# In the final projection x is added behind the joins instead of ahead of them, and the first gate block takes its units in another order

## The chip, the core and the metric

The kernel runs on one core of a Trainium2 chip. The metric is device time in microseconds: 2481.99 us, the median of three runs (2481.8 to 2482.37). One further execution was profiled; its trace is read below. TensorE (PE) multiplies matrices and loads weights beside that (PEld), VectorE (DVE) and ScalarE (ACT) do elementwise work, GpSimd (POOL) and SyncE (SP) only issue transfers in the part that matters here.

## The reference

One decoder layer on x (256 tokens, 4096 channels), in float32. What matters here are its last steps:

```python
proj = rmsnorm(h, g_pre) @ w_in          # ..., merge_a, merge_b are the last 2 x 4096 columns
...
merged = sigmoid(merge_a) * (o_a @ p_a) + sigmoid(merge_b) * (o_b @ p_b)
h = h + merged @ w_o                     # the final projection: x is added to it
```

## The kernel before

Every float32 product is made of three passes: both operands are split into a high part, which ACT rounds to the matmul type (`whi`, `whs`), and a low part, which DVE gets by subtraction (`wlo`, `wls`); PE then multiplies high by high, low by high and high by low (`mm3`, lines 106 to 108).

The second half of the kernel ("wide") streams the merge gates' columns of w_in, then p_a and p_b, then w_o. It goes in blocks of 1024 output columns: seven gate blocks, four blocks each of p_a and p_b, and four of w_o (cb = 0 to 3). A block's inner dimension is cut into 16 pairs of 128-row tiles, and each pair is one unit. A unit `p5` multiplies pair 5 plainly: 24 matmuls, one split of 2048 columns on DVE. A unit `s4` multiplies pair 4 in Winograd's way: 21 matmuls, but DVE first makes sums of weights (lines 1231 to 1233) and has more to split. `k1` or `k14` is no matmul: it packs the left operand of a pair, that is, makes the sums that the s units of that pair need, and overwrites a part of the pair's operand by a difference (`pack`, lines 1088 to 1098). After its pack the pair can't be multiplied plainly any more.

A list written by hand gives the order of the units of each block; `mixed` is the usual one. Work is emitted with a look-ahead: before PE's unit i come the splits of unit i+2 (`prep`), and the loads of units i+3 to i+5 on the SP queue into three buffers `wraw`. The split tiles `whi` and `wlo` have three buffers too. Each engine executes its own list in order.

A block fills eight accumulator banks of 512 columns: four for plain and late Winograd products (`c`), four for the Winograd products that several outputs share (`s`). Consecutive blocks swap the two sets. After the block's last s unit `sums_early` combines the s banks into four SBUF tiles `ev`, one per quarter of the output. After the last unit the c banks are added to them by a join: ACT copies a bank to a tile `evc` (two buffers) and POOL issues a transfer that accumulates it into `ev` (lines 1301 and 1302). The join of the quarters 0 follows the last unit's first half, the join of the quarters 1 comes two units later. The next block's first s unit needs the banks that this frees: it is the third unit (`p3 p5 s0`).

In the gate blocks `ev` then goes through a sigmoid and is stored. In the w_o blocks x is added: `add_x` (line 1385) issues on POOL's queue a transfer that accumulates 128x512 of x from HBM into `ev`. It stands at the end of `sums_early`, so ahead of the joins of the same four tiles; accumulations into one tile go one after another. `finish` (three units after the block's end) stores the four tiles, on POOL too. The last w_o block has no join: DVE adds the bank (`sum_late`) and SP stores.

Of the kernel before, what the change touches and what calls it, by code (L numbers as in the profile page):

```python
# [37 lines left out]
def kernel(ctx: ExitStack, tc: tile.TileContext, x, positions, g_pre, w_in, g_q_lat,  # L38
# [1004 lines left out]
    QUARTERS = [(m, h) for m in range(2) for h in range(2)]  # L1043
# [88 lines left out]
    def block(w, c0, order, end, npairs=16, base=0, sets="cs"):  # L1132

        seq = [(u[0], int(u[1:])) if isinstance(u, str) else u for u in order]
        b = {"w": w, "c0": c0, "end": end, "base": base, "sets": sets, "on": set(), "c": None, "s": None, "ev": None}
        prods = [i for i, u in enumerate(seq) if u[0] in "sp"]
        last_s = max([i for i in prods if seq[i][0] == "s"], default=None)
        for i, (kind, p) in enumerate(seq):
            sched.append({"kind": kind, "p": p, "b": b if kind in "sp" else None, "last_s": i == last_s,
                          "last": i == prods[-1]})  # L1140
# [22 lines left out]
    def raw_dma(i):  # L1163
        if i >= len(sched) or i in asked:
            return
        asked.add(i)
        u = sched[i]
        kind, p, b = u["kind"], u["p"], u["b"]
        if kind not in "spgm":
            return  # L1170
        t = raws[i] = wraw()
        if kind in "gm":
            src = go_d[p // 2][:, 8 * (p % 2):8 * (p % 2) + 8, :] if kind == "g" else mt_d[:, 8 * p:8 * p + 8, :]
            nc.sync.dma_start(flat(t), src.rearrange("p k t -> p (k t)"))
            return
        for kk in range(2):
            q = 1 - kk if kind == "s" else kk
            row = (2 * p + kk) * P
            nc.sync.dma_start(flat(t[:, 2 * q:2 * q + 2, :]), b["w"][row:row + P, b["c0"]:b["c0"] + 1024])
# [103 lines left out]
    def sums_early(b):  # L1283
        e = b["ev"] = ev_tiles()
        s = b["s"]
        v = nc.vector.tensor_tensor
        nc.scalar.copy(e[0, 0], s["p1"])
        v(e[0, 1], s["p6"], e[0, 0], op=ALU.add)
        v(e[1, 0], s["p7"], e[0, 1], op=ALU.add)
        v(e[0, 1], s["p5"], e[0, 1], op=ALU.add)  # L1290
        v(e[1, 1], s["p5"], e[1, 0], op=ALU.add)

    def sum_late(b, m, h, cs=slice(0, 512)):
        e = b["ev"][m, h]
        nc.vector.tensor_tensor(e[:, cs], b["c"][m, h][:, cs], e[:, cs], op=ALU.add)

    def join(b, m):

        for h in range(2):
            t = F["pb"].tile([P, 512], F32, name="evc", bufs=2)  # L1300
            nc.scalar.copy(t, b["c"][m, h])
            nc.gpsimd.dma_start(b["ev"][m, h], t, accum_op=ALU.add)
# [4 lines left out]
    def end_sig(d, c0):  # L1307
        def end(b):
            def finish(m):
                for h in range(2):  # L1310
                    e = b["ev"][m, h]
                    nc.scalar.activation(e, e, AF.Sigmoid, scale=r[:, m:m + 1])
                    nc.gpsimd.dma_start(sig_d[d][m * P:(m + 1) * P, c0 + 512 * h:c0 + 512 * h + 512], e)

            later.append((2, lambda: join(b, 1)))
            later.append((3, lambda: finish(0)))
            later.append((5, lambda: finish(1)))
        return end
# [3 lines left out]
    for n, (d, cb) in enumerate(gates):  # L1322
        order = mixed
        if n == 0:
            order = "p3 p5 s0 p7 s2 p9 k1 s4 p11 s6 s8 p13 s10 s1 s12 s14 p15".split()
        if n == len(gates) - 1:
            order = mixed[:15] + ["g0", "p15"]
        block(w_in, (C_MA, C_MB)[d] + 1024 * cb, order, end_sig(d, 1024 * cb), sets=("cs", "sc")[n % 2])
# [24 lines left out]
    def transpose_merged(cb):  # L1353
        banks = bank_set("c")
        e = F["merged"]
        t = F["merged_t"] = F["pb"].tile([P, 4, 512], F32, name="mt")
        for j2 in range(4):
            for a in range(2):
                for m in range(2):
                    j = 2 * j2 + a  # L1360
                    nc.tensor.transpose(banks[j2][:, a * S + m * P:a * S + (m + 1) * P],
                                        e[m, j // 4][:, (j % 4) * P:(j % 4 + 1) * P], ident)
            nc.scalar.copy(t[:, j2, :], banks[j2])
        if cb < 3:
            nc.gpsimd.dma_start(mt_d[:, 8 * cb:8 * cb + 8, :].rearrange("p k t -> p (k t)"), flat(t))
# [15 lines left out]
    def at_out(ap, c0, m, h):  # L1381
        return ap[m * P:(m + 1) * P, c0 + 512 * h:c0 + 512 * h + 512]

    def add_x(b, m, h):
        nc.gpsimd.dma_start(b["ev"][m, h], at_out(xf, b["c0"], m, h), accum_op=ALU.add)

    def end_out(b):
        def finish():
            for q in QUARTERS:
                nc.gpsimd.dma_start(at_out(of, b["c0"], *q), b["ev"][q])  # L1390

        later.append((2, lambda: join(b, 1)))
        later.append((3, finish))

    for cb in range(4):
        order = mixed
        if cb == 0:
            order = "p3 p5 t3 p7 p9 d3 s0 s1 p11 s2 s4 p13 s6 s8 p14 s10 s12 p15".split()
        elif cb == 1:
            order = mixed[:4] + ["k14"] + mixed[4:]  # L1400
        elif cb == 3:
            order = "p3 p5 s0 s1 p7 s2 s4 p9 s6 s8 p11 s10 s12 s14 p13 p15".split()
        block(w_o, 1024 * cb, order, end_out if cb < 3 else None, sets=("sc", "cs")[cb % 2])

    def on_unit(u):
        b = u["b"]
        if u["p"] == 4 and (b["w"] is p_a or b["w"] is p_b):
            d = 0 if b["w"] is p_a else 1
            F["sig", d] = load_sig(d, b["c0"] // 1024)

    def open_pb(n):
        if n:
            F["pbs"].close()
        else:
            F["py"] = ctx.enter_context(tc.tile_pool(name="sumpool2", bufs=1, side="right"))
        F["pbs"] = ctx.enter_context(ExitStack())
        F["pb"] = F["pbs"].enter_context(tc.tile_pool(name=f"wide2{n}", bufs=1, side="right"))

    def run_wide():
        open_pb(0)  # L1420
        first = {id(w): next(i for i, u in enumerate(sched) if u["b"] is not None and u["b"]["w"] is w)
                 for w in (p_a, w_o)}
        for i, u in enumerate(sched):
            b = u["b"]
            if i == first[id(p_a)] + 5:
                open_pb(1)
            if i == first[id(w_o)] + 4:
                open_pb(2)
            if b is not None:
                on_unit(u)  # L1430
            prep(i + 2)
            for j in range(3, 6):
                raw_dma(i + j)
            for n, f in list(later):
                later.remove((n, f))
                if n > 1:
                    later.append((n - 1, f))
                else:
                    f()
            if u["kind"] == "t":  # L1440
                transpose_merged(u["p"])
            elif u["kind"] == "s":
                unit_s(i, u)
                if u["last_s"]:
                    sums_early(b)
                    if b["w"] is w_o:
                        for q in QUARTERS:
                            add_x(b, *q)
            elif u["kind"] == "p" and u["last"] and b["end"] is None:
                def after(m, h):  # L1450
                    for q in range(2) if (m, h) == (1, 1) else (None,):
                        cs = slice(0, 512) if q is None else slice(256 * q, 256 * q + 256)
                        sum_late(b, m, h, cs)
                        nc.sync.dma_start(at_out(of, b["c0"], m, h)[:, cs], b["ev"][m, h][:, cs])

                unit_p(i, u, after)
            elif u["kind"] == "p" and u["last"] and b["w"] in (w_in, w_o):
                unit_p(i, u, lambda m, h, b=b: join(b, 0) if (m, h) == (0, 1) else None)
            elif u["kind"] == "p":
                unit_p(i, u)  # L1460
            if b is not None and u["last"] and b["end"] is not None:
                b["end"](b)
            for d in (raws, tops, los, hits, lots):
                d.pop(i, None)
# [14 lines left out]
    drain()  # L1479
    st_stack.close()  # L1480
    run_wide()


# [41 lines left out]
```

## Time and profile before

| | |
|---|---|
| median of three runs | 2481.99 us |
| the profiled execution | 2481.01 us |
| its span, first to last instruction | 2479.2 us |
| first gate block on PE | 1209.44 to 1293.84 us of the span |
| w_o block 0 ends, block 1 begins on PE | about 2219.1 us |
| PE busy | 2459.3 us |

A row of the timeline gives start, duration, engine, line, operation, tiles out and in, and in brackets the engine's idle time before it and what ended that. Matmuls overlap: in a row of them one starts every 0.23 us and each is shown 0.39 us long, so an idle gap shown is shorter than the time lost.

### The profile page before, as it was taken

The numbers are of one execution on the slowest core, as the hardware profiler recorded it, in microseconds if no ns is written. First come the engines' busy times: TensorE is split into PE (matmuls) and PEld (weight loads), VectorE is DVE, ScalarE is ACT, GpSimd is POOL, SyncE is SP. The second block draws the span as 40 slices with busy tenths as digits, with TensorE's granted clock in tenths as the row PEclk, the third lists the DMA queues.
The fourth block names the chain that finished last, engine by engine and source line by source line (L and its number), as shares of the span: only waits on it lengthen the run. The fifth ranks groups of instructions, "written<-read, shape, count | busy, mean of one in ns | idle before, by whom it ended". The sixth has DMA issues, their size and how long they took to land.

```text
span 2479.2 us, 31343 instructions
## 1 busy us (share of the span) xinstructions
PE 2459.3 (99%) x11760; PEld 2054.3 (83%) x11760; DVE 1817.1 (73%) x2075; ACT 1358.5 (55%) x1675; POOL 149.0 (6%) x199
## 2 busy tenths in 40 slices
PE   9999999999999999999999999999999999999999
PEld 7988888888888888888878888888888888887787
DVE  5676696655666656655899999999855446899888
ACT  6555555555665565554556665566543334555554
POOL 2000000000000000000000000000000000000110
PEclk9999999999999999999999999999999999999999
DMA  8655565566666666667666776777787667677875
GB/s 249 185 167 162 167 180 162 161 188 182 181 189 178 179 186 177 185 183 204 221 213 229 253 232 222 237 234 246 243 300 238 200 229 243 214 230 224 254 237 171
DMA packets 208552, 516.68 MB, mean 208 GB/s; under 512 B 26068, under 2 KB 39248, under 8 KB 207120
## 3 DMA queue, kind: packets, MB, share of 16 engines
q1 hardware_dynamic: 190816, 468.25, 60.1%
q0 software_dynamic: 17536, 46.42, 7.0%
q8 instruction: 92, 1.51, 0.2%
q14 instruction: 60, 0.49, 0.1%
q10 hardware_dynamic: 48, 0.02, 0.0%
HBM read 482.11 MB, written 22.02 MB: 203 GB/s over the span
## 4 chain that ended last, share of the span: by engine, by line
PE 83%; issue 7%; DVE 5%; DMA 4%; ACT 1%; POOL 0%; SPq 0%; DVEq 0%; ACTq 0%; POOLq 0%
PE acc L106 20%; PE acc L108 20%; PE acc L107 20%; PE at L106 4%; PE at L107 4%; PE at L108 4%; PE tr L108 3%; PE tr L107 3%; PE tr L106 3%; DVE wlo L1054 2%; PE tr L129 2%; DMA ev<-evc 1%; DVE wls L1054 1%; DMA ev<-in_x 1%; DVE wsum L1231 1%
## 5 line engine op out<-in xcount | busy, mean ns | idle before, releaser
L237 DVE TENSOR_TENSOR lo<-raw,hi 128x1024 fp32r<-128x1024 f32 (+3 forms) x400 | 476.2, 1192 | 373.3 <-ACT hi L229 364.0
L1054 DVE TENSOR_TENSOR wlo<-wraw,whi 128x2048 fp32r<-128x2048 f32 (+2 forms) x338 | 561.5, 1669 | 189.6 <-ACT whi L1053 188.0
L1053 ACT CAST whi<-wraw 128x2048 fp32r<-128x2048 f32 (+2 forms) x338 | 474.9, 1413 | 393.3 <-PE at L107 140.7
L229 ACT CAST hi<-raw 128x1024 fp32r<-128x1024 f32 (+3 forms) x400 | 408.2, 1024 | 285.6 <-PE acc L107 258.2
L106 PE MATMUL acc<-hi,h 128*128 128x512 f32 (+1 forms) x1404 | 554.5, 395 | 0.0
L108 PE MATMUL acc<-lo,h 128*128 128x512 f32 (+1 forms) x1404 | 546.2, 389 | 0.0
L107 PE MATMUL acc<-hi,l 128*128 128x512 f32 (+1 forms) x1404 | 545.0, 388 | 0.2
L108 PEld LDWEIGHTS acc<-lo,h 128*128 128x128 f32 x1404 | 263.5, 188 | 56.0 <-DVE lo L237 0.4
L107 PEld LDWEIGHTS acc<-hi,l 128*128 128x128 f32 x1404 | 264.0, 188 | 48.0 <-DVE l L85 1.0
L106 PEld LDWEIGHTS acc<-hi,h 128*128 128x128 f32 x1404 | 263.7, 188 | 46.7
L106 PE MATMUL acc<-whi,h 128*128 128x512 f32 x686 | 267.5, 390 | 0.0
L108 PE MATMUL acc<-wlo,h 128*128 128x512 f32 x686 | 267.1, 389 | 0.0
L107 PE MATMUL acc<-whi,l 128*128 128x512 f32 x686 | 267.1, 389 | 0.0
L1053 ACT CAST whs<-wsum 128x1536 fp32r<-128x1536 f32 x98 | 145.3, 1482 | 108.0 <-DVE wsum L1232 105.9
L1054 DVE TENSOR_TENSOR wls<-wsum,whs 128x1536 fp32r<-128x1536 f32 x98 | 171.6, 1751 | 0.0
L108 PE MATMUL tr<-wlo,h 128*128 128x512 f32 x394 | 153.6, 390 | 0.3 <-DVE wlo L1054 0.3
L106 PE MATMUL tr<-whi,h 128*128 128x512 f32 x394 | 153.5, 390 | 0.0
L107 PE MATMUL tr<-whi,l 128*128 128x512 f32 x394 | 153.5, 390 | 0.0
L108 PEld LDWEIGHTS acc<-wlo,h 128*128 128x128 f32 x686 | 128.9, 188 | 26.8
L106 PEld LDWEIGHTS acc<-whi,h 128*128 128x128 f32 x686 | 128.9, 188 | 26.7
L107 PEld LDWEIGHTS acc<-whi,l 128*128 128x128 f32 x686 | 128.9, 188 | 26.6
L106 PE MATMUL at<-whi,h 128*128 128x512 f32 x350 | 136.4, 390 | 0.0
(338 smaller groups left out, 3352.9 us busy)
## 6 DMA issues: line engine op xcount, KB each, us to landing
raw<-in_w_in SPq DMA_DIRECT2D x335, 512.0 KB, 3.7
wraw<-in_w_in SPq DMA_DIRECT2D x224, 512.0 KB, 4.6
wraw<-in_w_o SPq DMA_DIRECT2D x128, 512.0 KB, 5.2
wraw<-in_p_a SPq DMA_DIRECT2D x64, 512.0 KB, 5.0
wraw<-in_p_b SPq DMA_DIRECT2D x64, 512.0 KB, 5.1
raw<-in_w_uq SPq DMA_DIRECT2D x32, 384.0 KB, 3.2
ev<-evc POOLq DMA_DIRECT2D x40, 256.0 KB, 6.5
raw<-in_w_ukv SPq DMA_DIRECT2D x16, 512.0 KB, 3.9
```

Of the source, the lines that this page charges most:

```text
L106: nc.tensor.matmul(o, ah, bh, start=start, stop=False)
L107: nc.tensor.matmul(o, al, bh, start=False, stop=False)
L108: nc.tensor.matmul(o, ah, bl, start=False, stop=stop)
L129: nc.tensor.transpose(tr[:, a * S + m * P:a * S + (m + 1) * P], src_of(a, m), ident)
L229: nc.scalar.copy(t[:, ks, :width(i)], raws[i][:, ks, :width(i)])
L237: nc.vector.tensor_tensor(t[:, ks, :wd], raws[i][:, ks, :wd], his[i][:, ks, :wd].bitcast(F32), op=ALU.subtract)
L1053: nc.scalar.copy(hi, src)
L1054: nc.vector.tensor_tensor(lo, src, hi.bitcast(F32), op=ALU.subtract)
L1231: v(t[:, 0:2, :], raw[:, 3, None, :].to_broadcast([P, 2, 512]), raw[:, 1:3, :], op=ALU.subtract)
```

## The change

It has two parts. In the w_o blocks 0 to 2 the four `add_x` leave `sums_early`'s place and go into `finish`, behind both joins and just ahead of the stores. The last block, which has no `finish`, keeps them where they were. And the first gate block has another list of units: pair 1 is now multiplied plainly, as its first unit, before its pack; the pack k1 moves from the seventh place to the fourth; the other s units alternate with p units.

```diff
     for n, (d, cb) in enumerate(gates):
         order = mixed
         if n == 0:
-            order = "p3 p5 s0 p7 s2 p9 k1 s4 p11 s6 s8 p13 s10 s1 s12 s14 p15".split()
+            order = "p1 p3 s0 k1 p5 s2 p7 s4 p9 s6 p11 s8 s10 p13 s12 s14 p15".split()
...
     def end_out(b):
         def finish():
+            for q in QUARTERS:
+                add_x(b, *q)
             for q in QUARTERS:
                 nc.gpsimd.dma_start(at_out(of, b["c0"], *q), b["ev"][q])
...
                 if u["last_s"]:
                     sums_early(b)
-                    if b["w"] is w_o:
+                    if b["end"] is None:
                         for q in QUARTERS:
                             add_x(b, *q)
```

On POOL's queue this is w_o block 0 before (`ev` the four quarters, `evc` the copies of the banks, `in_x` x):

```order
L1385 DMA ev_18085<-in_x 128x512
L1385 DMA ev_18086<-in_x 128x512
L1385 DMA ev_18087<-in_x 128x512
L1385 DMA ev_18088<-in_x 128x512
L1302 DMA ev_18085<-evc 128x512
L1302 DMA ev_18086<-evc 128x512
L1302 DMA ev_18087<-evc 128x512
L1302 DMA ev_18088<-evc 128x512
L1390 DMA out<-ev_18085 128x512
L1390 DMA out<-ev_18086 128x512
L1390 DMA out<-ev_18087 128x512
L1390 DMA out<-ev_18088 128x512
```

And the same block now:

```order
L1302 DMA ev_18078<-evc 128x512
L1302 DMA ev_18079<-evc 128x512
L1302 DMA ev_18080<-evc 128x512
L1302 DMA ev_18081<-evc 128x512
L1385 DMA ev_18078<-in_x 128x512
L1385 DMA ev_18079<-in_x 128x512
L1385 DMA ev_18080<-in_x 128x512
L1385 DMA ev_18081<-in_x 128x512
L1392 DMA out<-ev_18078 128x512
L1392 DMA out<-ev_18079 128x512
L1392 DMA out<-ev_18080 128x512
L1392 DMA out<-ev_18081 128x512
```

The four transfers of x went behind the four of the joins; the stores now wait for them.

On DVE, in the first gate block, this stood behind s0 before: the split of p7, then s2 (line 1231 begins an s unit), the split of p9, and only then the pack of pair 1 (line 1088; `h_126` and `l_127` are pair 1's operand).

```order
L1054 TENSOR_TENSOR wlo<-wraw,whi 128x512
L1054 TENSOR_TENSOR wlo<-wraw,whi 128x2048
L1231 TENSOR_TENSOR wsum<-wraw 128x1024
L1232 TENSOR_TENSOR wsum<-wraw,wsum 128x512
L1233 TENSOR_TENSOR wraw<-wraw,wsum 128x512
L1054 TENSOR_TENSOR wlo<-wraw,whi 128x1536
L1054 TENSOR_TENSOR wls<-wsum,whs 128x1536
L1054 TENSOR_TENSOR wlo<-wraw,whi 128x512
L1054 TENSOR_TENSOR wlo<-wraw,whi 128x2048
L1088 TENSOR_TENSOR wsum<-h_126,l_127 128x512
L1073 TENSOR_TENSOR wsum<-wsum 128x128
L1074 TENSOR_TENSOR wsum<-wsum 128x128
```

And now, from the same place:

```order
L1054 TENSOR_TENSOR wlo<-wraw,whi 128x512
L1088 TENSOR_TENSOR wsum<-h_126,l_127 128x512
L1073 TENSOR_TENSOR wsum<-wsum 128x128
L1074 TENSOR_TENSOR wsum<-wsum 128x128
L1075 TENSOR_TENSOR wsum<-wsum 128x128
L1076 TENSOR_TENSOR wsum<-wsum 128x128
L1096 TENSOR_TENSOR l_127<-wsum,h_126 128x128
L1098 TENSOR_TENSOR xl_11108<-wsum,xh_11107 128x384
L1054 TENSOR_TENSOR wlo<-wraw,whi 128x2048
L1231 TENSOR_TENSOR wsum<-wraw 128x1024
L1232 TENSOR_TENSOR wsum<-wraw,wsum 128x512
L1233 TENSOR_TENSOR wraw<-wraw,wsum 128x512
```

The pack follows s0 at once, ahead of the next p unit and of s2; further down, one s unit's instructions became one split of 2048 columns.

## Rows read from the trace of the kernel before

**Rows 1.** The page, part 1: busy time of each engine, share, instructions.
```profile
PE 2459.3 (99%) x11760; PEld 2054.3 (83%) x11760; DVE 1817.1 (73%) x2075; ACT 1358.5 (55%) x1675; POOL 149.0 (6%) x199
```
**Rows 2.** Waits of PE over the span: total us, times, longest.
```profile
PE acc L106 <- ACT evc L1301: 6.3, 2, 4.7
PE acc L108 <- DVE wls L1054: 2.8, 2, 1.5
PE at L106 <- ACT evc L1301: 2.0, 2, 1.7
```
**Rows 3.** Timeline of PE, first gate block, third matmul of unit s12.
```profile
1275.63 0.39 PE L107 MATMUL acc<-whs,xl 128*128 128x512 f32 x1
1277.39 0.50 PE L108 MATMUL acc<-wls,xh 128*128 128x512 f32 x1 [1.37 <-DVE wls L1054]
```
**Rows 4.** Timeline of DVE, first gate block.
```profile
1218.07 2.29 DVE L1054 TENSOR_TENSOR wlo<-wraw,whi 128x2048 fp32r<-128x2048 f32 x1 [1.26 <-ACT whi L1053]
1222.50 1.23 DVE L1231 TENSOR_TENSOR wsum<-wraw 128x1024 f32<-128x1024 f32 x1 [2.14 <-DMA wraw<-in_w_in]
...
1231.24 0.68 DVE L1088 TENSOR_TENSOR wsum<-h,l 128x512 f32<-128x512 f32 x1
...
1234.27 1.23 DVE L1231 TENSOR_TENSOR wsum<-wraw 128x1024 f32<-128x1024 f32 x1
...
1243.01 1.22 DVE L1231 TENSOR_TENSOR wsum<-wraw 128x1024 f32<-128x1024 f32 x1
```
**Rows 5.** Timeline of PE, w_o block 1: in s0, at s1, s2 and s4.
```profile
2231.15 0.39 PE L108 MATMUL acc<-wls,xh 128*128 128x512 f32 x1
2236.24 0.80 PE L106 MATMUL acc<-whs,h 128*128 128x512 f32 x1 [4.71 <-ACT evc L1301]
...
2242.54 0.39 PE L106 MATMUL acc<-whs,xh 128*128 128x512 f32 x1
...
2252.76 0.39 PE L106 MATMUL acc<-whs,xh 128*128 128x512 f32 x1
...
2257.97 0.39 PE L108 MATMUL acc<-wls,xh 128*128 128x512 f32 x1
```
**Rows 6.** Stretches: length, each engine's busy time, granted clock, DMA share, GB/s.
```profile
2215.00:2230.00 15.00, 15.00 (x67) 12.41 (x67) 14.39 (x14) 9.79 (x9) 5.22 (x6) 1.00 1.04 285
2236.20:2242.20 6.00, 5.96 (x14) 4.70 (x15) 4.39 (x5) 2.40 (x3) 2.52 (x4) 0.50 0.96 264
2300.00:2330.00 30.00, 28.02 (x123) 22.55 (x122) 25.95 (x23) 16.90 (x16) 9.15 (x12) 1.00 1.00 266
```
**Rows 7.** Timeline of POOL, w_o block 0's first join.
```profile
2224.49 0.85 POOL L1302 DMA_DIRECT2D ev<-evc  x1 [5.24 <-DMA ev<-in_x]
```
**Rows 8.** Line 1302 from 2200 to 2410 us: from issue to landing.
```profile
DMA to landing us min/median/max: 5.7/7.4/10.0
```
**Rows 9.** Timeline of ACT, w_o block 1, the second join of block 0.
```profile
2233.14 0.59 ACT L1301 COPY evc<-acc 128x512 f32<-128x512 f32 x1 [3.07 <-DMA ev<-evc]
2235.60 0.59 ACT L1301 COPY evc<-acc 128x512 f32<-128x512 f32 x1 [1.88 <-DMA ev<-evc]
```
**Rows 10.** Timeline of DVE, w_o block 1: end of k14, p7, s2, s4.
```profile
2236.42 0.29 DVE L1096 TENSOR_TENSOR l<-wsum,h 128x128 fp32r<-128x128 f32 x1 [1.94 <-ACT h L1093]
...
2238.63 2.29 DVE L1054 TENSOR_TENSOR wlo<-wraw,whi 128x2048 fp32r<-128x2048 f32 x1 [1.24 <-ACT whi L1053]
...
2244.05 1.76 DVE L1054 TENSOR_TENSOR wlo<-wraw,whi 128x1536 fp32r<-128x1536 f32 x1 [0.54 <-ACT whi L1053]
...
2252.25 1.75 DVE L1054 TENSOR_TENSOR wls<-wsum,whs 128x1536 fp32r<-128x1536 f32 x1
```
**Rows 11.** Timeline of ACT, w_o block 2, first copy of block 1's second join.
```profile
2318.55 0.59 ACT L1301 COPY evc<-at 128x512 f32<-128x512 f32 x1 [1.29 <-DMA ev<-evc]
```
**Rows 12.** Timeline of PE, w_o block 2, first matmul of s0.
```profile
2319.19 0.50 PE L106 MATMUL at<-whs,xh 128*128 128x512 f32 x1 [0.31 <-ACT evc L1301]
```
**Rows 13.** Weight loads (line 1179) from 2150 to 2440 us: from issue to landing.
```profile
DMA to landing us min/median/max: 4.0/5.4/10.3
```

## The prediction

> **What bounds the kernel now.** The page comes first: PE is busy for 99% of the span [rows 1], so only two things can shorten it, less work on PE or fewer holes between its matmuls. The view of PE's waits lists the holes [rows 2]: four in which PE waits for ACT's copies `evc` (6.3 + 2.0 us) and two for the Winograd low part `wls` from DVE (2.8 us). The timeline places them. The two on DVE lie in the first gate block [rows 3], the four on `evc` at the first s unit of w_o blocks 1, 2 and 3 [rows 5, 12]. All are places that the change touches. Seven gate blocks end with the same join and no x, and none of these four holes is theirs.
>
> A hole costs more than the gap shown. In a row of matmuls one starts every (2257.97 - 2252.76) / 23 = 0.2265 us [rows 5] and each is drawn 0.39 us long. In rows 3 two starts lie 1.76 us apart, so 1.53 is lost where the row says 1.37; the matmul that waited is drawn 0.50 long and the next one starts 0.11 later. So gap + 0.27 is lost. The longest hole costs still more: from 2231.15 to 2242.54 are 11.39 us for 16 starts, which take 3.62 elsewhere; 7.77 are lost, though the gap is 4.71 [rows 5]. Behind it the granted clock is 0.50, the 1.2 GHz level, until about 2242.2 [rows 6].
>
> **The first gate block.** Lost now: 2.8 + 2 x 0.27 = 3.4. PE pays for the new list: pair 1 as p takes 24 matmuls and not 21, 3 x 0.2265 = 0.7. On DVE, s4 and p11 together run from 1234.27 to 1243.01, 8.74; a p unit is 2.2 (2.29 less the overlap), so an s unit 6.5 [rows 4]. Turning s1 into p1 saves 4.3 of DVE. The pack k1 takes 1234.27 - 1231.24 = 3.0 [rows 4]; it now stands directly behind s0, where DVE idled 1.26 and then 2.14 for weights that had not arrived [rows 4]. It needs no load, so that idle time covers it. It must wait until PE has read pair 1 in p1, the block's first unit: from 1209.44, 24 matmuls end near 1214.9, before the pack begins (s0 ends on DVE at 1218.07 - 1.26 = 1216.8). The price: p5 comes behind the pack and ACT's part of it, at about 1221.4 (1216.8 + 3.0, and 1.6 for ACT's split), where p7 stood at 1218.1; s2 follows at 1223.6 instead of 1222.5. PE needs s2's `wls` at 1209.44 + (2 x 24 + 21 + 24 + 2) x 0.2265 = 1231.0; DVE, which takes 6.0 from a unit's start to the end of its `wls` (6.5 less the last quarter's split), has it at 1229.6. From there s and p alternate: 6.5 + 2.2 = 8.7 on DVE against 45 x 0.2265 = 10.2 on PE, so the lead grows. At s14 DVE stands 3.0 + 4.3 - 1.1 = 6.2 better, more than the 3.4 by which PE comes earlier without the holes. Both go: 3.4 - 0.7 = 2.7 won. Bounds: 3.4 lost and 0.7 paid give -0.7 (holes stay) to +2.7; I take 2.7, since the lead at the tightest unit is 1.4.
>
> **x behind the joins.** The transfers of x are no fewer: 12 of the 16 move by some 15 us, past the joins on POOL's queue. Their only consumer now is the stores, and those have some 70 us until the next block wants `ev`. Before, the first join's transfer stood on POOL for 5.24 us until x had landed [rows 7], so it could have gone at 2219.25. It lands 7.4 later, 10.0 at most [rows 8], the second one 0.9 behind: 2227 to 2230. ACT's next copy wants that buffer at 2233.14 - 3.07 = 2230.07 [rows 9]. So it no longer waits: two copies of 0.59 end at 2231.25, and PE wants them at 2231.15 + 0.23 = 2231.38. The hole goes, with a margin of 0.1.
>
> What is late next is DVE. PE would be 7.77 earlier, but DVE's idle time there was short [rows 10]: of 1.94 at the end of k14 about 0.3 stays (ACT's own copy has to run), the 1.24 before p7 stays (ACT splits p7 behind k14's copies, as now), and the 0.54 before s2 goes with PE's earlier release of the buffer. So DVE moves 1.6 + 0.5 = 2.2 earlier. The tightest unit is s4: its `wls` ends at 2254.0 [rows 10], PE reads it at 2257.97 [rows 5], a lead of 3.9. PE can gain 3.9 + 2.2 = 6.1 before it waits for s4, so some 1.7 come back as a new hole on `wls`. Later units of the block don't bind: behind s4 units alternate with p. Bounds 3.9 (DVE doesn't move) and 7.8 (no new hole); I take 6.1.
>
> At blocks 2 and 3 the holes cost 2.0 + 2 x 0.27 = 2.5 and (6.3 - 4.7) + 0.27 = 1.9 [rows 2]. In block 2 ACT was free at 2318.55 - 1.29 = 2317.26 [rows 11], PE wanted the copy at 2318.7 (2319.19 less the 0.31 and the 0.16 of overlap) [rows 12]: with the buffer free both copies are in time, and DVE, which then idled behind ACT's two waits, gains more than PE does. Bounds 0 and 4.4 together; I take 4.4.
>
> The one remaining wait could cost clock too. The stretch 2300 to 2330, with PE gaps of 0.3 and 1.7, was granted 1.00 throughout [rows 6], so a hole of 1.7 at s4 should not halve it. The Trainium skill (TensorE: Matmul & The Clock Gate, What's actually happening) says that the throttled state is the default and that activity lifts it. By that page alone a hole at s4 could cost a throttled stretch as well, about 2.9 us by the row of the 4.71 gap (7.77 - 4.71 - 0.16), and the time would be 2471.7; the row decides, and I give this 0.05, inside the forecast's range.
>
> **The sum.** 2.7 + 6.1 + 4.4 = 13.2. The profiled execution took 2481.01 (span 2479.2); it would take 2467.8. The median shown is 0.98 above it, so I forecast 2468.8.
>
> **Rivals.**
> 1. DVE takes more back. If ACT's split of p7 comes no earlier, w_o block 1 gives 3.9; if DVE then enters block 2 late too, the copies behind its s1 are late and the 2.5 there go. 13.2 - 2.2 - 2.5 = 8.5: 2473.5. For it: DVE was busy for 14.39 of the 15.00 us from 2215 to 2230 [rows 6], so little idle time is there to be won. Against: the idle times in rows 10 name ACT, whose waits the change removes [rows 9].
> 2. The change does not do what it says: the copies wait for the joins' own transfers, not for x. Then the projection gives about 2 and the gate block 2.7: 2477.3, which is no change. For it: the join's transfer takes 7.4 by itself [rows 8], and the margin at block 1 is 0.1. Against: 5.24 of waiting on x is plain in rows 7, and the gate blocks' joins show no such hole.
> 3. Slower: x collides with the weights. The stretch with x in it has its DMA engines at 1.04 [rows 6], and the loads' landing goes from 5.4 to 10.3 at worst [rows 13]. Now x runs with the stores behind it, at the s units, where DVE takes most. If one load per block comes 10.3 - 5.4 = 4.9 late on PE and the clock falls for another 2.9, three blocks lose 23.4; against the 13.2 that is +10.2: 2492.2. It decides from the point at which a load lands later than its unit's lead; a load is issued three units ahead, at least 13 us of DVE's work, so 10.3 still fits. The Trainium skill (DMA: Bandwidth & Descriptors, Issuing engines are not separate DMA queues) speaks for this rival: transfers of all queues run on the same 16 engines and interleave, so that moving x on POOL's queue only moves the load. The trace agrees with the 1.04.
>
> **How the numbers follow.** Forecast 0.70, rival 1 0.18, rival 2 0.07, rival 3 0.05. About 0.2%, 5 us, is what a measurement of this kernel can tell from no change. Forecast and rival 1 are faster by more: 0.88; same 0.07; slower 0.05. Low end: no new hole at s4 gives 1.7 more, 2467.1, less 1 for the scatter: 2466. High end: rival 1 and a microsecond, 2474.5.
>
> **What would show it.** PE's waits for `evc` gone from the view, and no stretch at 0.50 near 2236. POOL's rows of x behind the joins', and no wait for x before line 1302. A new gap on `wls` of 1 to 2 us some 30 us into w_o block 1. No `wls` gap in the first gate block, which takes 81.6 us on PE instead of 84.4. Wrong would be: `evc` gaps of over 1 us at s0, ACT waiting for weights in the blocks 1 to 3, or a hole over 3 us at s4.

## The result and the profile after

| | before | after |
|---|---|---|
| median, six runs each | 2481.94 us | 2469.15 us |
| lowest to highest | 2480.1 to 2484.11 | 2467.76 to 2470.5 |
| the profiled execution | 2481.01 | 2468.7 |
| its span | 2479.2 | 2466.9 |

The ratio is 0.9948, with a 95% interval of 0.9935 to 0.9961: 12.8 us faster. The forecast was 2468.8. The page, part 1, of the kernel after [rows 1]:

```profile
PE 2456.9 (100%) x11763; PEld 2054.7 (83%) x11763; DVE 1813.0 (73%) x2070; ACT 1355.9 (55%) x1673; POOL 149.0 (6%) x199
```

PE executes three matmuls more, and the span is 12.3 us shorter: what went are holes. PE's waits over the span, as total us, times, longest [rows 2]:

```profile
PE acc L108 <- DVE wls L1054: 1.8, 2, 1.3
PE at L329 <- DVE nhalf L85: 1.2, 1, 1.2
PE at L108 <- DVE wls L1054: 0.9, 1, 0.9
```

No row names `evc`. The last two rows stand the same in the trace of before. Of the first, one wait is new and foreseen, at s4 of w_o block 1; the other, at s14 of the last block, is new and was not foreseen. The timeline of PE there [rows 5]:

```profile
2247.74 0.39 PE L107 MATMUL acc<-whs,xl 128*128 128x512 f32 x1
2249.44 0.50 PE L108 MATMUL acc<-wls,xh 128*128 128x512 f32 x1 [1.31 <-DVE wls L1054]
...
2445.87 0.39 PE L107 MATMUL acc<-whs,xl 128*128 128x512 f32 x1
2446.70 0.50 PE L108 MATMUL acc<-wls,xh 128*128 128x512 f32 x1 [0.44 <-DVE wls L1054]
```

By the rule of the prediction (gap + 0.27) they cost 1.58 and 0.71. The clock, by stretches [rows 6]; the columns are length, busy time and instructions of PE, PEld, DVE, ACT and POOL, granted clock, DMA share, GB/s:

```profile
2225.00:2255.00 30.00, 28.69 (x127) 23.43 (x126) 27.99 (x31) 16.66 (x16) 7.42 (x10) 1.00 0.93 268
2236.20:2242.20 6.00, 6.00 (x28) 4.99 (x27) 5.93 (x6) 3.37 (x3) 2.00 (x3) 1.00 1.09 268
2300.00:2330.00 30.00, 30.00 (x134) 24.85 (x133) 28.86 (x26) 17.95 (x16) 7.35 (x10) 1.00 0.94 259
```

In the six microseconds in which the view counted 14 matmuls at 0.50 it now counts 28 at 1.00; in the stretch of block 2 PE has no gap. The first gate block in the same view, after (1209 to 1294 us):

```profile
1209.00:1294.00 85.00, 85.00 (x377) 70.41 (x376) 80.09 (x72) 48.52 (x41) 2.54 (x3) 1.00 0.67 224
```

PE has 377 matmuls there and not one gap; before it had 361 in the same 85 us. From its first matmul at 1210.24 to the next block's first at 1291.84 it takes 81.60 us, before 84.39.

POOL's queue at w_o block 1 shows the move [rows 7]:

```profile
2215.87 1.79 POOL L1302 DMA_DIRECT2D ev<-evc  x2 [145.08 <-ACT evc L1301]
2228.61 1.72 POOL L1302 DMA_DIRECT2D ev<-evc  x2 [10.95 <-ACT evc L1301]
2229.68 3.29 POOL L1385 DMA_DIRECT2D ev<-in_x  x3
2236.46 0.85 POOL L1385 DMA_DIRECT2D ev<-in_x  x1 [3.49 <-DMA ev<-evc]
2239.50 0.58 POOL L1392 DMA_DIRECT2D out<-ev  x1 [2.19 <-DMA ev<-in_x]
```

The joins wait for ACT's copies alone, and the first goes at 2215.87 where it went at 2224.49. What waits for transfers now are x and the stores, for which nobody waits. ACT's copies of the second join [rows 9]:

```profile
2227.74 1.06 ACT L1301 COPY evc<-acc 128x512 f32<-128x512 f32 x2
```

They run back to back, with no wait for a buffer.

### The profile page after: what moved, and what is told of

Its sections match the earlier page's. It is cut to its first block, busy times and chain, and to the rows that moved or that the text cites. A ratio compares the mean times of both kernels' runs of the same rounds, so it can differ in the third digit from the quotient of the medians.

```text
span 2466.9 us, 31331 instructions
## 1 busy us (share of the span) xinstructions
PE 2456.9 (100%) x11763; PEld 2054.7 (83%) x11763; DVE 1813.0 (73%) x2070; ACT 1355.9 (55%) x1673; POOL 149.0 (6%) x199
```

## The experiments

Each kernel was timed against the kernel before on the same chip; that kernel's median there was 2481.5 to 2482.3 us. The first four take the change apart.

**Only the new place of x** (the kernel after, with the old list):

```diff
         if n == 0:
-            order = "p1 p3 s0 k1 p5 s2 p7 s4 p9 s6 p11 s8 s10 p13 s12 s14 p15".split()
+            order = "p3 p5 s0 p7 s2 p9 k1 s4 p11 s6 s8 p13 s10 s1 s12 s14 p15".split()
```

> Only the part on x: the first gate block keeps its old list. Theory (each hole is its own, the terms add): the three joins' holes go, 6.1 + 2.5 + 1.9 less the 0.6 of a new hole at s14 of the last block, so about 10 us under the kernel before; the two wls holes of the first gate block stay (gaps of about 1.4 each). Rival (the holes are one budget of VectorE time: VectorE stays late from the gate block on and takes back in w_o what the copies give): under 8 us, with larger wls holes in w_o block 1 than the 1.3 seen after the change.

Measured: 2474.02 us (2472.15 to 2474.09), ratio 0.9962 [0.9948, 0.9976], so 7.5 under before by the medians and 9.4 by the ratio, where the sum has 10.5; the interval, 6.0 to 12.9, does not decide. The trace does. The timeline of PE, gate block and w_o block 1:

```profile
1277.06 0.50 PE L108 MATMUL acc<-wls,xh 128*128 128x512 f32 x1 [1.30 <-DVE wls L1054]
1283.59 0.50 PE L108 MATMUL acc<-wls,xh 128*128 128x512 f32 x1 [1.47 <-DVE wls L1054]
...
2232.28 0.50 PE L106 MATMUL acc<-whs,h 128*128 128x512 f32 x1 [1.08 <-ACT evc L1301]
...
2252.87 0.50 PE L108 MATMUL acc<-wls,xh 128*128 128x512 f32 x1 [1.38 <-DVE wls L1054]
```

The gate holes stay, as they should, and the hole at s4 is hardly larger than the 1.31 of the kernel after, against the rival. But at s0 of block 1 a gap of 1.08 is left; that is the place whose margin the prediction gave as 0.1. PE's row names ACT's copies, yet these waited for no transfer (timeline of ACT):

```profile
2216.60 1.91 ACT L1053 CAST whi<-wraw 128x2048 fp32r<-128x2048 f32 x1 [4.50 <-DVE ev L1291]
...
2229.26 1.48 ACT L1053 CAST whs<-wsum 128x1536 fp32r<-128x1536 f32 x1 [3.14 <-DVE wsum L1232]
...
2231.17 1.06 ACT L1301 COPY evc<-acc 128x512 f32<-128x512 f32 x2
```

They run back to back, behind a cast that waited for DVE's sums, and the lateness begins at the block's first split. Ahead of that split ACT idled 4.50 us here, and 4.11, 4.62 and 4.38 in the three profiles below that have such a gap (one without x, two with k14 later). In the five profiles with a gap of 0.19 or less at this place it idled 2.95 to 3.32. Seven of these nine rows name the weights of that unit, whose load is issued ahead of any x of the projection. So what is left at s0 is a late load of weights, and not a join; why it is late in some kernels is open. By late starts PE lost 10.8 us behind 1200 us, where it lost 18.9 before: 8.1 less, about the 10.5 without 1.4 for this gap and 0.9 for one of 0.69 at s14 of the last block.

**Only the new list** (the kernel before, with the first hunk of the diff alone):

```diff
-            order = "p3 p5 s0 p7 s2 p9 k1 s4 p11 s6 s8 p13 s10 s1 s12 s14 p15".split()
+            order = "p1 p3 s0 k1 p5 s2 p7 s4 p9 s6 p11 s8 s10 p13 s12 s14 p15".split()
```

> Only the new list of the first gate block; x stays ahead of the joins. Theory: 3.4 of holes go, 0.7 of TensorE work comes, 2.7 us less than before, and the evc holes of w_o blocks 1 to 3 stay as they were (4.7, 0.3 + 1.7, 1.6), with the half clock behind the first. Rival (a hole closed in the gate block opens again later, since VectorE is then late in the next blocks): no change in time, a new wls hole in one of the later gate blocks.

Measured: 2479.51 (2476.02 to 2487.12), ratio 0.9991 [0.9981, 1.0001]: 2.0 less, with an interval that reaches to nothing. The gate block lost its holes here too, but the profiled execution, the longest of the ten, has gaps by the copies of 4.28 at 2236, of 3.51 and 0.51 at 2321 and of 3.23 at 2411, the last two places worse than before. PE's waits:

```profile
PE acc L106 <- ACT evc L1301: 7.5, 2, 4.3
PE at L106 <- ACT evc L1301: 4.0, 2, 3.5
```

The rival's new `wls` hole in a later gate block did not come. By the medians the list's gain is smaller alone than behind the other part, where it is 3.5 (0.9962 against 0.9948) to 4.9 (2474.02 against 2469.15). The intervals overlap, and the one profile is that of the longest run; that some of the gain is given back in the projection is likely, but not shown.

**No x at all in w_o blocks 0 to 2** (so the output lacks x there):

```diff
         def finish():
             for q in QUARTERS:
-                add_x(b, *q)
-            for q in QUARTERS:
                 nc.gpsimd.dma_start(at_out(of, b["c0"], *q), b["ev"][q])
```

> The changed kernel without the transfers of x in w_o blocks 0 to 2, so these blocks' outputs lack x. Theory (moved x is hidden but crowds the weight loads): ScalarE's waits for weights in w_o fall from 27 us to near the 4.7 of before, the hole of 0.4 at s14 of the last block goes, the hole of 1.3 at s4 of block 1 stays, and the time falls by 0.5 to 1 us only. Rival (x still costs the path several us, at the stores or by late weights): 3 us or more less than the changed kernel.

Measured: 2468.93 (2468.61 to 2470.36), ratio 0.9943: the twelve moved transfers cost the kernel after 0.2 us by the medians and 1.2 by the ratios, no more than the runs scatter. The theory's other points: the gap at s14 of the last block is gone, as it said, and the one at s4 stays (1.48); ACT's waits for weights fall to 13.1 us only, not to near 4.7. The gap of 0.69 at s0 of block 1 is the late load again.

**x behind the joins in block 0 only:**

```diff
         def finish():
-            for q in QUARTERS:
-                add_x(b, *q)
+            if b["c0"] == 0:
+                for q in QUARTERS:
+                    add_x(b, *q)
...
-                    if b["end"] is None:
+                    if b["w"] is w_o and b["c0"] > 0:
                         for q in QUARTERS:
```

> The changed kernel, but in w_o blocks 1 and 2 x goes back ahead of the joins. Theory (the terms add, block 0's is 6.1 because its hole also halves the clock): the evc gaps of 0.3 + 1.7 and 1.6 are back at w_o blocks 2 and 3 and cost 4.4, time about 4 us above the changed kernel, 9 under the one before; granted clock 1.00 throughout. Rival (TensorE, now 6 us earlier, meets the late copies with a longer gap): the gap at block 2 grows to over 4 us, the clock falls there to 0.50, and the time is 8 us or more above the changed kernel.

Measured: 2479.68 (2476.49 to 2483.2), ratio 0.9989 [0.9980, 0.9999]: 10.5 over the kernel after (10.2 by the ratios), where the terms for blocks 2 and 3 are 4.4. The theory that the terms add fell. The rival was right on the time and the clock, but not on the size of the gap at block 2, which it put at over 4. The block-2 gaps on PE:

```profile
2314.02 0.79 PE L106 MATMUL at<-whs,xh 128*128 128x512 f32 x1 [2.49 <-ACT evc L1301]
2316.68 0.79 PE L106 MATMUL at<-whs,xh 128*128 128x512 f32 x1 [1.01 <-ACT evc L1301]
```

They were 0.31 [rows 12] and 1.67 before, and 3.30 stands at block 3 for 1.64. Behind both the clock falls; here is the stretch behind the first (PE alone; granted clock, DMA share, GB/s):

```profile
2300.00:2330.00 30.00, 26.50 (x105) 0.89 0.96 266
2314.00:2322.00 8.00, 6.97 (x19) 0.60 1.00 260
```

So is the size of a hole chance, or set by the program? **The kernel before, again,** with a second profile:

> The kernel before, unchanged, for a second profile. Theory: the holes by the copies of the joins differ from one execution to the next, as they end with DMA landings that scatter by some us; so the gaps at blocks 2 and 3 are not again those of the first profile (losses of 2.5 and 1.9 us there), at least one of the three gaps differs by over 1 us, and the losses from 1200 us on add up to another sum than 18.9 us by more than 2 us, the span moving with it. Rival: the sizes are set by the program; each gap is the same within 0.5 us and only the start-up scatters.

Measured: 2482.79. PE's waits:

```profile
PE acc L106 <- ACT evc L1301: 6.4, 2, 4.9
PE acc L108 <- DVE wls L1054: 2.5, 2, 1.5
PE at L106 <- ACT evc L1301: 2.5, 2, 1.6
```

These are almost rows 2. The gaps: 4.86 for 4.71; 0.88 + 1.59 for 0.31 + 1.67; 1.49 for 1.64; all that PE lost behind 1200 us, by late starts, is 19.3 for 18.9. So the theory, that chance moves a gap by over 1 us, is not borne out by these two executions, and the rival's half a microsecond is missed by little. But two executions of nearly the same length do not show that the program alone sets the holes. The kernels that share the projection of the one before, and differ in the first gate block's list only, had 4.28 (above), 2.96 and 3.55 (below) at block 1, and 3.23, 2.01 and 2.62 at block 3. And twenty runs of the kernel before took 2479.07 to 2486.27 us, a spread of 7.2 us, while the wide stage began within 3.6 us in all profiles. How much of a hole is the program's and how much the execution's stays open. Where the larger holes with x behind in block 0 only come from can be read off block 2. POOL issues x, then the first join; ACT then copies into the freed buffer. First the kernel before, second profile (POOL, then ACT):

```profile
2302.86 0.88 POOL L1385 DMA_DIRECT2D ev<-in_x  x1 [56.80 <-DVE ev L1288]
2311.33 0.86 POOL L1302 DMA_DIRECT2D ev<-evc  x1 [4.35 <-ACT whi L1053]
...
2319.19 0.58 ACT L1301 COPY evc<-at 128x512 f32<-128x512 f32 x1 [1.87 <-DMA ev<-evc]
```

And the kernel with x behind in block 0 only:

```profile
2295.55 0.88 POOL L1385 DMA_DIRECT2D ev<-in_x  x1 [48.13 <-DVE ev L1288]
2304.94 0.86 POOL L1302 DMA_DIRECT2D ev<-evc  x1 [5.26 <-DMA ev<-in_x]
...
2313.39 0.59 ACT L1301 COPY evc<-at 128x512 f32<-128x512 f32 x1 [2.84 <-DMA ev<-evc]
```

The first join's wait in the kernel before names a cast of ACT; x of its tile was 7.9 us under way and landed at 2310.8, half a microsecond ahead of it. The chain of two transfers took 2319.19 - 2302.86 = 16.33 there and 17.84 here, 8.5 + 7.9 against 9.4 + 8.4. PE, from the same issue to its own want, takes 16.1 (2319.83 - 0.88 - 2302.86) and 16.0 (2314.02 - 2.49 - 2295.55). With a copy of 0.59 ahead of PE this makes gaps of 0.8 and 2.5, as the rows of PE show. Both pieces of the chain took longer, and each microsecond is a microsecond of gap, with the clock on top. Why they landed later when block 1 had no hole is open: from 2300 to 2330 the DMA engines are busy for 0.96 of the time here and 0.99 there.

**Which x does it?** The copies have two buffers, and the first join, that of the upper quarters, holds both. Half of x ahead again, that of the lower quarters:

```diff
         def finish():
-            for q in QUARTERS:
+            for q in QUARTERS[:2]:
                 add_x(b, *q)
...
-                    if b["end"] is None:
-                        for q in QUARTERS:
+                    if b["w"] is w_o:
+                        for q in QUARTERS if b["end"] is None else QUARTERS[2:]:
```

> The kernel after, with x of the two lower quarters added ahead of the joins again in blocks 0 to 2 of the final projection; only the two upper quarters, whose joins come first, get x behind them. Theory: the copies of a join wait for the two buffers that the first two joins hold, and these wait only for x of their own quarters; with that behind, the lower quarters' x has landed long before their joins, so no evc gap above 0.5 us appears in blocks 1 to 3 and the time is that of the kernel after, 2469 us (2468 to 2471). Rival: any x in POOL's queue ahead of the joins delays them, as the issue waits for DVE's early sums and the transfers share the engines: evc gaps of 1 to 3 us return in at least two of the three blocks, with half clock behind the larger ones, and the time is 2474 to 2480 us.

Measured: 2469.68 (2467.45 to 2471.31), ratio 0.9949 [0.9932, 0.9966]: the time of the kernel after. PE's waits for the copies:

```profile
PE acc L106 <- ACT evc L1301: 0.6, 1, 0.6
```

The gaps were 0.12 at block 1, too short for the view, none at block 2, and 0.64 at block 3 (0.14 more than the theory allowed). The rival was right in so far as x ahead slows joins that do not wait for it: from issue to landing the twelve joins took 8.7 us in the median and 13.4 at most, where those of the kernel after took 6.9 and 9.6. The mirror, with `QUARTERS[2:]` behind and `QUARTERS[:2]` ahead:

> The mirror of the half: x of the two upper quarters is added ahead of the joins in blocks 0 to 2 of the final projection, that of the two lower quarters behind them. As many bytes ahead as in the half before. Theory: the joins of the upper quarters come first and hold both copy buffers until x of their own quarters has landed, so the gaps by the copies return: over 1.5 us in at least two of blocks 1 to 3, half clock behind those over 2.4 us, and the time is 2474 to 2480 us. Rival: it is the number of transfers ahead that counts, and two of 256 KB are few enough: no gap over 0.7 us, 2469 to 2471 us as with the other half.

Measured: 2473.77 (2472.78 to 2477.59), ratio 0.997 [0.9958, 0.9981], some 4 to 5 over the kernel after. Gaps of 0.19, 3.56 and 1.02: less than the theory, which wanted two over 1.5, and more than the rival, which allowed 0.7. The profile is that of the longest of the six runs, the one of the kernel before this that of the shortest of four; the times of the two kernels do not overlap. Block 2 shows the mechanism bare (POOL, ACT, PE):

```profile
2297.60 0.88 POOL L1385 DMA_DIRECT2D ev<-in_x  x1 [49.46 <-DVE ev L1288]
2299.11 0.86 POOL L1385 DMA_DIRECT2D ev<-in_x  x1 [0.63 <-DVE ev L1290]
2307.09 0.85 POOL L1302 DMA_DIRECT2D ev<-evc  x1 [7.12 <-DMA ev<-in_x]
2309.74 0.85 POOL L1302 DMA_DIRECT2D ev<-evc  x1 [1.80 <-DVE wsum L1231]
...
2317.14 0.59 ACT L1301 COPY evc<-at 128x512 f32<-128x512 f32 x1 [4.21 <-DMA ev<-evc]
...
2317.78 0.50 PE L106 MATMUL at<-whs,xh 128*128 128x512 f32 x1 [3.56 <-ACT evc L1301]
```

POOL waits 7.12 for the first x. The second one, issued at 2299.11, takes 10.1 us, and the second join goes half a microsecond behind its landing. ACT's second copy waits 4.21 for that join, and PE 3.56 for ACT. With as many bytes ahead, the upper half brings holes and the lower half none worth the name: it is x of the quarters that join first. All four ahead cost more (x ahead in blocks 1 and 2 or in all three left the time some 10 over the kernel after), so the number counts too.

**Which half of the list does it?** Two kernels from the one before. k1 early, without p1:

```diff
-            order = "p3 p5 s0 p7 s2 p9 k1 s4 p11 s6 s8 p13 s10 s1 s12 s14 p15".split()
+            order = "p3 p5 s0 k1 p7 s2 p9 s4 p11 s6 s8 p13 s10 s1 s12 s14 p15".split()
```

> The kernel before with one unit of the first gate block's list moved: k1 stands right behind s0 instead of behind p9; p1 is not added, and x is added ahead of the joins as before. Theory: in the old list DVE reaches the sum of s4 late because it also forms the stationary sums of k1 between s2 and s4; with k1 ahead of s2 DVE does them where it was idle behind s0, so the gap at s4 goes (PE lost 1.7 us there), but s2 is not earlier relative to its use, and the gap at s2 or at the unit behind it stays (another 1.7 us): time about 2480.2 us, 1.5 to 2 under the kernel before, at least one wls gap over 1 us left in the block. Rival: k1 alone pulls both forward, both gaps vanish and p1 does nothing: 3 us under before. Second rival: k1 ahead of s2 delays s2, a gap of 2 us or more at s2, and the time is that of before or above.

p1 at the head, k1 late:

```diff
-            order = "p3 p5 s0 p7 s2 p9 k1 s4 p11 s6 s8 p13 s10 s1 s12 s14 p15".split()
+            order = "p1 p3 s0 p5 s2 p7 k1 s4 p9 s6 p11 s8 s10 p13 s12 s14 p15".split()
```

> The kernel before with p1 put at the head of the first gate block's list and k1 left near its old place, behind p7; x ahead of the joins as before. Theory: p1 gives PE more columns before s2 and s4 are wanted, but DVE's own queue is not shorter: the sums of k1 still stand between s2 and s4, so the gap at s4 stays or moves (about 1 to 1.7 us), the one at s2 goes; about 1.5 us under the kernel before. Rival: the length of PE's work ahead is all that counts, both gaps go and the time is that of the whole new list, 2 us under before or more.

Measured: 2478.28 (2477.33 to 2482.39), ratio 0.9986 [0.9977, 0.9995], and 2479.28 (2475.46 to 2482.4), 0.9985 [0.9976, 0.9994]; the two can't be told apart by time. By the trace the block takes 81.99 us on PE with k1 early (one gap of 0.78 is left, at s14, 0.2 under what the theory expected to see) and 81.60, with no gap, with p1: as much as with both. Both expectations put the two gaps at s2 and s4; they stood at s12 and s14. Here the rival of the second was right, and the sums of k1 between s2 and s4 do no harm once p1 is there. In both the projection's holes stand, though not in the sizes of before (2.96, 0.56 + 1.67 and 2.01; 3.55, 0.30 + 1.68 and 2.62).

**The new hole at s4.** In w_o block 1 of the kernel after, k14 was put later:

```diff
         elif cb == 1:
-            order = mixed[:4] + ["k14"] + mixed[4:]
+            order = "p3 p5 s0 s1 p7 s2 p9 k14 s4 p11 s6 s8 p13 s10 s12 s14 p15".split()
```

> The kernel after, with the unit k14 of block 1 of the final projection moved from behind s1 to behind p9, and p9 ahead of s4. Theory: the only hole over 1 us that the change left behind 1215 us outside the merges is DVE's, at s4 of this block (gap 1.31 us, 1.58 us lost), since DVE forms the sums of k14 before those of s4; with p9 (16 matmuls, 3.6 us of PE) between and the sums of k14 behind s2's, the wls of s4 is there in time: the hole goes, nothing takes its place, 1.2 to 1.6 us under the kernel after, about 2467.8 us. Rival: the columns of k14 covered something else (the copies of the first join at s0, or the sums of s2): a new hole of 0.7 to 1.5 us at s0 or s2 of the block takes its place and the time is that of the kernel after within 0.5 us, 2469 us.

Measured: 2472.23 (2471.54 to 2473.4), ratio 0.9959 [0.9947, 0.9971], 2.2 over the kernel after timed beside it (below), worse than the rival said. PE's waits:

```profile
PE acc L108 <- DVE wls L1054: 2.9, 3, 1.5
PE acc L106 <- ACT evc L1301: 1.2, 1, 1.2
PE at L106 <- ACT evc L1301: 0.4, 1, 0.4
```

The gap at s4 shrank to 0.67, but one of 1.46 came at s14 of the block, and the copies at its s0 are 1.21 late; 0.74 stands in the last block. A hole at s0 is what the rival named, but it is not k14's, which stands behind s0 in both lists: ACT's first split of the block came late here, and in time in the kernel after (second row):

```profile
2215.16 1.91 ACT L1053 CAST whi<-wraw 128x2048 fp32r<-128x2048 f32 x1 [4.62 <-DMA wraw<-in_w_o]
...
2213.18 1.91 ACT L1053 CAST whi<-wraw 128x2048 fp32r<-128x2048 f32 x1 [2.95 <-DMA wraw<-in_w_o]
```

So the 1.5 us that PE loses at s0 can't be put down to k14. DVE has little slack in this block: what the pack takes is missing at one s unit or at another, and the later it stands, the fewer p units are left to make up for it. That last reason is argued from the order, not shown. (The expectation gives p9 16 matmuls and 3.6 us; a p unit has 24, which take 5.4.)

Both edits together:

> The kernel after with both edits that runs so far or the trace pointed to: x of the two lower quarters ahead of the joins, that of the upper two behind them, and k14 of block 1 behind p9. Theory: the two add up, as the first changes no wait of PE (2469.7 us beside 2469.2) and shortens only POOL's row of x behind the joins, and the second takes away the hole at s4: 2468 us, 1 us under the kernel after. Rival: the lower quarters' x takes DMA time from the first joins when k14 no longer lies between, an evc hole of 1 us or more comes at s0 of block 1, and the time is 2469.5 to 2471 us.

Measured: 2471.57 (2471.34 to 2474.55), 0.9961 [0.9949, 0.9973], 1.6 over the kernel after by the medians; gaps of 0.97 at s0, 0.87 and 1.46 on `wls`. The time is 0.6 above the rival's range, and its hole of about 1 at s0 came, but not by its reason: the kernel without the half shows the same holes, and the first split came late here too (4.38).

**The kernel after, again,** beside these:

> The kernel after, unchanged, beside the two others, for a time on the same chip and a second profile. Theory: the sizes of the holes are set by the program, so the one at s4 of block 1 is again 1.3 us within 0.3 us, that at s14 of the last block stays under 1 us, and no evc gap over 0.3 us appears; 2469 us (2467.5 to 2470.5). Rival: the copies at s0 of block 1 were ready by a margin of 0.1 us only, so an evc gap of 0.5 to 1.3 us stands there this time, and the time is 2470 us or more.

Measured: 2470.01 (2467.99 to 2471.33), ratio 0.9949 [0.9938, 0.9961]. The gaps: 1.46 at s4, 0.61 at s14, none by the copies. No kernel tried is faster than it by more than the scatter.

## Why the prediction was right

**The bound.** Only holes and work on PE could change the time. With late starts summed behind 1200 us, PE lost 18.9 us before and 5.3 after; the difference, 13.6, less 0.7 for three matmuls and 0.8 by which the wide stage began later, is 12.1 beside 12.3 of span.

**The gate block** was to win 2.7 and take 81.6 us instead of 84.4; it takes 81.60 instead of 84.39. The DVE rows of the kernel after [rows 4]:

```profile
1217.65 0.69 DVE L1088 TENSOR_TENSOR wsum<-h,l 128x512 f32<-128x512 f32 x1
...
1221.91 2.29 DVE L1054 TENSOR_TENSOR wlo<-wraw,whi 128x2048 fp32r<-128x2048 f32 x1 [1.25 <-ACT whi L1053]
1224.12 1.22 DVE L1231 TENSOR_TENSOR wsum<-wraw 128x1024 f32<-128x1024 f32 x1
...
1228.38 1.75 DVE L1054 TENSOR_TENSOR wls<-wsum,whs 128x1536 fp32r<-128x1536 f32 x1
```

p5 was put at 1221.4 and s2 at 1223.6; they stand at 1221.9 and 1224.1, and `wls` ends at 1230.1 for 1229.6: all by the 0.8 or less that the stage began later. What the prediction did not see is that what the two halves of the new list give overlaps: p1 alone does all of it, k1 alone all but 0.4.

**w_o block 1** was to win 6.1, as 7.8 less a new hole of 1.7 at s4. The hole cost 1.58, so 6.2 were won; a repeat showed a gap of 1.46. DVE's rows were to move 2.2 earlier at s4: its `wls` ended at 2254.0 [rows 10] and ends now at 2247.63 + 1.75 = 2249.4, 4.6 earlier; 2.2 of that DVE had already where the pack of k14 begins (2232.61 before, 2230.39 after), and 2.4 are left for the 2.2. The step that a hole of this size keeps the clock is right too: 1.00 through 2225 to 2255 above. The Trainium skill (TensorE: Matmul & The Clock Gate, What's actually happening) makes the throttled state the default that activity lifts; the trace agrees in so far as 0.50 stood in block 1 behind the 4.71 [rows 6] and not behind the 1.31. A longer gap is not all that decides, as the last section shows.

**Blocks 2 and 3** were to win 4.4, all of their holes; all are gone. As a price of their own the 4.4 did not hold: with x ahead in blocks 1 and 2, 10.5 was lost. The prediction read each hole as a fixed sum; the two executions of the kernel before lost nearly the same (19.3 and 18.9), but a hole is PE's wait for a chain of two transfers, and it had another size in most kernels that were changed ahead of it. The two parts of the change alone fall short of both together as well (7.5 + 2.0 by the medians, 9.4 + 2.2 by the ratios, against 12.8), though by hardly more than the intervals. The total of 13.2 came out since the change takes all of the holes away at once.

**Not foreseen:** 0.6 at s14 of the last block (0.71 for 0.11). It goes with x: a gap of 0.44 to 0.74 stands there in the four profiles with x of all quarters behind the joins in block 2, and none of 0.1 in the others, which have x or half of it ahead, or none in block 2. With it the terms are 2.7 + 6.2 + 4.4 - 0.6 = 12.7; less the late start of 0.8 that is 11.9 beside the 12.3 measured on the two profiled executions.

**The rivals.** The first (DVE takes back) was right about DVE: moving k14 finds no slack there. But nothing of its 4.7 was paid, as DVE's idle times went the way of the forecast (0.38 is left at the pack, 1.25 stays before p7, none is left before s2) and block 2 has no hole. The second (the copies wait for the joins' own transfers) did not come, as no gap by the copies is left in either profile of the kernel after. The first two joins took 5.0 and 7.9 us to land, the last at 2224.4, and ACT's next copies began at 2227.74 without waiting for them. The margin of 0.1 measured 0.4: the copies end at 2228.80, and the first matmul that needs them starts at 2229.16. It is a margin of ACT against PE, and the prediction had no term for what uses it up, the late load: a gap of 1.08 with the old list, 0.69 with no x at all, 1.21 and 0.97 with k14 later, 0.12 or less in the four other profiles that have x of the first quarters behind in block 0. The third (x collides with the weights) happens, and is hidden but for the 0.6 in the last block. Waits from 2150 us on, after:

```profile
ACT whi L1053 <- DMA wraw<-in_w_o: 27.0, 14, 4.3
POOL out L1392 <- DMA ev<-in_x: 24.4, 12, 2.7
DVE wsum L1231 <- DMA wraw<-in_w_o: 3.1, 4, 2.0
```

ACT's wait for weights was 4.7 us in three places before; the prediction named such waits as a sign that it would be wrong, and this sign was badly chosen: of the 27.0 us PE's rows show those 0.6, and without x in three blocks 13.1 of the 27.0 remain, at the same time of the kernel. The Trainium skill (DMA: Bandwidth & Descriptors, Issuing engines are not separate DMA queues) says that transfers run on the same 16 DMA engines and interleave, whichever engine issued them. The trace agrees with these waits, and the run without x prices what x adds to them at 0.2 to 1.2 us.

## What to carry to other kernels

A transfer that accumulates into a tile ahead of another on the same tile is a link in that one's chain; if only the store needs its result, issue it last, or at least for the tiles whose buffers are wanted first. Read how long the chain takes against how long the bound engine takes to the same point, rather than the size of the hole that shows: here 16.3 against 16.1 and 17.8 against 16.0 us, with a copy behind, were gaps of 0.9 and 2.5. The row of a wait names the last link of its chain only: PE's holes at s0 name ACT's copies in every kernel here, and behind them stood a chain of transfers in one and a late load of weights in another. And test parts of a change together with the rest, since a hole taken away in one block may come back in the next.

## What was not expected of the hardware

- x behind the joins takes long to land: 9.3 to 12.3 us, median 10.8, for 256 KB, where the weights' 512 KB had a median of 5.9 in about the same stretch. Off the path it costs nothing.
- Nearly the same total gap may or may not bring the lower clock: 0.31 + 1.67 in block 2 kept 1.00 [rows 6], 0.88 + 1.59 in the repeat left 0.94 over the same 30 us, that is about 30 x 0.06 / 0.5 = 3.6 us at the 1.2 GHz level. Of the single gaps in the projection, those up to 2.01 us kept 1.00 in every profile, and behind each one from 2.62 us up a stretch at 0.50 stands.
- The time spreads more with x ahead in two or three blocks: 5 to 11 us from the fastest to the slowest of ten runs, against 2 to 4 in four to six runs with x of the first quarters behind.
